# Sum of reciprocals: one row's reciprocal as a power on GpSimd

## The chip, the cores and the metric

The kernel runs on one core of one Trainium2 chip (the other seven are not used). The metric is the device time of one execution in microseconds (us), smaller is better; the input of 67.1 MB is read from HBM once, and the result of 64 KB is written back. The engines are named as in the profile: PE (TensorE), DVE (VectorE), ACT (ScalarE), POOL (GpSimd), and SP, which only issues DMAs here.

## The reference

```python
def setup_inputs():
    batch, seq, dim = 32, 512, 1024
    return {"x": np.abs(np.random.randn(batch, seq, dim)).astype(np.float32) + 1e-6}

def reference(x):
    return np.sum(1.0 / x, axis=-1).astype(np.float32)
```

For each of the 16,384 rows of 1,024 positive fp32 numbers the sum of the reciprocals is wanted.

## The kernel before

The 16,384 rows lie on 128 partitions, 128 rows to a partition (F = 128), numbered 0 to 127 in the order of the work. "Row 1" is thus one tile of 128 x 1024, row 1 of each partition. The rows go through a ring of R = 46 slots in SBUF (`ring`, 4 KB of each partition for a slot); row r takes slot r % 46, so rows 46 and up have to wait until the row 46 earlier has been finished. Row 127 is cut in two halves, handled as pieces 127 and 128. The sums go into `sums`, 128 x 128, and to HBM in seven stores at the end.

The reciprocal is made in two steps: ScalarE's `Abs_reciprocal_sqrt` gives 1/sqrt(x), with the scale FIT, in place, and then some engine squares it and sums it over the row. There are several ways for the second step, and the kernel spreads the rows over them:

- Z: ScalarE squares the row and sums it by itself.
- G, then T: GpSimd multiplies the row by itself in place (L280), and VectorE sums it (`tensor_reduce`, L283).
- Q: VectorE multiplies and sums in one instruction (L240).
- B, later K and M: VectorE takes batch-norm statistics (L255), from which the sum of squares is worked out later.
- C: ScalarE squares the row without summing, and T sums it.
- U, P, L, E, R: the two halves of a row are added by PE into PSUM (U, L201) and multiplied by GpSimd (P, L194); ScalarE takes the inverse root of the product (L) and squares it (E, both L211); VectorE multiplies product and sum and adds up (R, L220). This uses 1/a + 1/b = (a + b) / (a b), and saves ScalarE half of the elements.

The order of all of this is written out by hand in the string PLAN. A token is a letter, a row, and `+n` for n rows at once: A0+2 is the inverse root of rows 0 and 1 on ScalarE, G1+3 the square of rows 1 to 3 on GpSimd, T2+2 the sums of rows 2 and 3. Dn loads the next n rows; all loads are issued from SP. Each engine handles its own tokens strictly in the order of PLAN. Waits between engines follow from `note`, which keeps a history of who read and wrote which part of which slot, and leaves out the waits that others imply. Before the plan, GpSimd gets EARLY = 13 idle instructions (`nop`).

At the front the first loads are D2, D12, D12, D9 and D11, which fill the 46 slots: rows 0 and 1, then 2 to 13, and so on. They are issued one right after the other. The next load, D10, stands in PLAN behind T6+4 and needs slots 0 to 9, so it waits until rows 0 to 9 are finished. ScalarE's queue begins A0+2, Z0, A2, A3, A4+3, A7, A8, A9; GpSimd's G1+3, G6+3, G9, G11; VectorE's T1, T2+2, T6+4. The identity matrix for PE is made on GpSimd by `make_identity` (masks.py) ahead of the plan; PE uses it first for U53.

Of the kernel before, what the change touches and what calls it, by code (L numbers as in the profile page):

```python
# [11 lines left out]
def kernel(  # L12
# [5 lines left out]
    nc = tc.nc  # L18
    f32 = mybir.dt.float32
    P = 128  # L20
    EARLY = 13
    D = 1024
    H = D // 2
    F = 128
# [14 lines left out]


    PLAN = """
        D2 D12 D12 D9 D11 A0+2 Z0 A2 A3 A4+3 G1+3 A7 A8 A9 G6+3 A10 T1 A11+3 T2+2 Z4 Z5 G9 Z10
        Z12 G11 T6+4 D10 A14 A15+2 G13 A17+3 G16 T11 T13 A20+4 G17 Q15 G19 T16+2 A24+2 G20 A26
        A27 G21 A28+2 G23+3 A30+2 T19+3 A32+3 Z14 D8 G26 C33 Z18 G27 Z22 Z29 G28 A35+2 G30+3
        T23+6 D8 A37+3 A40+4 G34+2 T30+2 A44+2 Z36 T32 G40 Z37 T33+3 D8 Z38 G44+2 U53@0 A46+2
# [33 lines left out]
    pool = ctx.enter_context(tc.tile_pool(name="pool", bufs=1))  # L79
# [6 lines left out]
    stat_rows = [i for lo, step, n in STATS for i in range(lo, lo + step * n, step)]  # L86
    stats = pool.tile([P, len(stat_rows), 2, 2, 3], f32)
    ident = pool.tile([P, P], f32)
    ps = pspool.tile([P, 8, H], f32)
    make_identity(nc, ident)  # L90

    def parse(tok):
        body, _, b = tok[1:].partition("@")
        r, _, n = body.partition("+")
        return tok[0], int(r), int(n or 1), int(b or 0)

    def place(u):
        return (u, 0, D) if u < NR else PIECES[u - NR]

    def area(u, n=1):  # L100
        r, at, w = place(u)
        if u >= NR:
            w, n = sum(place(i)[2] for i in range(u, u + n)), 1
        return ring[:, r % R : r % R + n, at : at + w]
# [36 lines left out]
    def rows(u, n=1):  # L141
        spaces = []
        for r, at, w in (place(i) for i in range(u, u + n)):
            spaces += [("row", r % R, i) for i in range(at, at + w, 128)]
        return spaces
# [12 lines left out]
    with tc.manual_schedule():  # L158
        for _ in range(EARLY):
            nc.gpsimd.nop(hint="idle", nofuse=True)  # L160
        for op, u, n, b in (parse(tok) for tok in PLAN):
            if op == "D":
                n, u = u, loaded
                while n:
                    r, at, w = place(u)
                    m = min(n, R - r % R, NR - u, HALF - r % HALF) if u < NR else n
                    k = m
                    if u >= NR:
                        w, k = sum(place(i)[2] for i in range(u, u + m)), 1
                    inst = nc.sync.dma_start(  # L170
                        out=area(u, m),
                        in_=x_v[r // HALF, :, r % HALF : r % HALF + k, at : at + w],
                    )
                    note("SP", inst, writes=rows(u, m))
                    u, n = u + m, n - m
                loaded = u
            elif op in "AC":
                inst = nc.scalar.activation(  # L178
                    out=area(u, n),
                    in_=area(u, n),  # L180
                    func=Arsqrt if op == "A" else Square,
                    scale=FIT if op == "A" else 1.0,
                )
                note("ACT", inst, writes=rows(u, n))
            elif op == "Z":
                r = place(u)[0]
                inst = nc.scalar.activation(  # L187
                    out=area(u), in_=area(u), func=Square, accum_out=sums[:, r : r + 1]
                )
                summed.add(r)  # L190
                note("ACT", inst, writes=rows(u))
            elif op == "P":
                slot[u], r = b, u % R
                inst = nc.gpsimd.tensor_tensor(  # L194
                    out=prod[:, b], in0=ring[:, r, :H], in1=ring[:, r, H:], op=mult
                )
                note("POOL", inst, rows(u), [("slot", b)])
            elif op == "U":
                bank[u], r = b, u % R
                for h in range(2):  # L200
                    inst = nc.tensor.matmul(  # L201
                        ps[:, b],
                        lhsT=ident,
                        rhs=ring[:, r, h * H : (h + 1) * H],
                        start=h == 0,
                        stop=h == 1,
                    )
                    note("PE", inst, half(u, h * H), [("bank", b)])
            elif op in "LE":
                pair = prod[:, slot[u]]  # L210
                inst = nc.scalar.activation(  # L211
                    out=pair,
                    in_=pair,
                    func=Arsqrt if op == "L" else Square,
                    scale=S * FIT if op == "L" else 1.0,
                )
                note("ACT", inst, writes=[("slot", slot[u])])
            elif op == "R":
                pair = prod[:, slot[u]]
                inst = nc.vector.tensor_tensor_reduce(  # L220
                    out=pair,
                    in0=pair,
                    in1=ps[:, bank[u]],
                    scale=S,
                    scalar=0.0,
                    op0=mult,
                    op1=add,
                    accum_out=sums[:, u : u + 1],
                )
                note("DVE", inst, [("bank", bank[u])], [("slot", slot[u])])  # L230
            elif op == "Q":
                r, at, w = place(u)
                joined = [u]
                while len(joined) < n:
                    joined += [i for i in range(NR, u) if place(i)[0] == r][-len(joined) :][:1]
                at -= sum(place(i)[2] for i in joined[1:])
                w += sum(place(i)[2] for i in joined[1:])
                row = ring[:, r % R, at : at + w]
                total = sums[:, r : r + 1]
                inst = nc.vector.tensor_tensor_reduce(  # L240
                    out=row,
                    in0=row,
                    in1=row,
                    scale=1.0,
                    scalar=total if r in summed else 0.0,
                    op0=mult,
                    op1=add,
                    accum_out=total,
                )
                summed.add(r)  # L250
                note("DVE", inst, writes=[s for i in joined for s in rows(i)])
            elif op == "B":
                i = stat_rows.index(u)
                for h in range(2):
                    inst = nc.vector.bn_stats(  # L255
                        out=stats[:, i, h], in_=ring[:, u % R, h * H : (h + 1) * H]
                    )
                    note("DVE", inst, reads=half(u, h * H), writes=[("stat", i)])
            elif op in "KM":
                lo, step, n = STATS[u]  # L260
                i = stat_rows.index(lo)
                part = stats[:, i : i + n]
                if op == "K":
                    mean = part[:, :, :, :, 1].rearrange("p f h e -> p (f h e)")
                    inst = nc.scalar.activation(  # L265
                        out=mean, in_=mean, func=Square, scale=float(H // 2) ** 0.5
                    )
                    engine = "ACT"
                else:
                    inst = nc.vector.tensor_reduce(  # L270
                        out=sums[:, lo : lo + step * (n - 1) + 1 : step],
                        in_=part[:, :, :, :, 1:].rearrange("p f h e k -> p f (h e) k"),
                        axis=mybir.AxisListType.XY,
                        op=add,
                    )
                    engine = "DVE"
                note(engine, inst, writes=[("stat", j) for j in range(i, i + n)])
            elif op == "G":
                row = area(u, n)
                inst = nc.gpsimd.tensor_tensor(out=row, in0=row, in1=row, op=mult)  # L280
                note("POOL", inst, writes=rows(u, n))
            elif op == "T":
                inst = nc.vector.tensor_reduce(  # L283
                    out=sums[:, u : u + n],
                    in_=area(u, n),
                    axis=mybir.AxisListType.X,
                    op=add,
                )
                note("DVE", inst, reads=rows(u, n))
            elif op == "O":  # L290
                for lo, hi in zip(STORES, STORES[1:]):
                    store(lo, hi)
        store(STORES[-1], F)
# [30 lines left out]
```

## Time and profile before

| what | value |
|---|---|
| median of 2 runs | 166.24 us (166.18 to 166.3) |
| span of the profiled execution, first to last instruction | 164.2 us |
| ACT busy | 145.7 us (89%) in 148 instructions |
| DVE busy | 115.9 us (71%) in 147 instructions |
| POOL busy | 108.8 us (66%) in 56 instructions |
| PE busy | 38.2 us (23%) in 68 matmuls |
| input queue | 67.18 MB, 96.3% of the span of 16 DMA engines |
| mean granted TensorE clock | 0.952 |

The span is what the profile can explain; the time of a run is some 2 us longer, since it also holds what lies before the first and after the last instruction. The busy time of an engine is summed over its instructions; the idle instructions (`nop`), semaphore waits and the issuing of DMAs are not counted as busy. A row of the timeline gives the start, the duration, the engine, the line of the code, the operation, output and input tile with their shapes, the number of instructions merged in it, and in brackets how long the engine idled before it and which engine's work ended that.

### The profile page before, as it was taken

What the parts mean: (1) busy time and instruction counts of PE and PEld (TensorE: products, weight loads), DVE (VectorE), ACT (ScalarE), POOL (GpSimd) and SP (SyncE); (2) the same over time, 40 slices, a digit from 0 to 9 for tenths busy, and PEclk for the clock granted to TensorE, in tenths of its full rate; (3) what the DMA queues carried; (4) which work ended last, traced back from release to release, by engine and by line L of the source; (5) the groups of instructions that cost most, each with busy time, mean ns of one, the idle gap of its engine ahead of it and who ended that gap; (6) DMA issues with size and microseconds to landing.
All of it is one profiled execution on the core that took longest, in us unless ns stands there. A gap on an engine that the chain in (4) does not pass through costs nothing.

```text
span 164.2 us, 640 instructions
## 1 busy us (share of the span) xinstructions
PE 38.2 (23%) x68; PEld 14.4 (9%) x68; DVE 115.9 (71%) x147; ACT 145.7 (89%) x148; POOL 108.8 (66%) x56
## 2 busy tenths in 40 slices
PE   0000000000000000053000000065908198699700
PEld 0000000000000000020000000032302033234200
DVE  0000003559927039999999999999698969999894
ACT  3600199999999999999999999999999999999994
POOL 1000069998999999999507979999926195477300
PEclk9999999999999999999999999999975859999985
DMA  5999899899989899999998998999999999999970
GB/s 188 463 539 407 383 395 563 383 431 431 463 351 527 351 479 409 391 455 431 391 503 383 431 463 381 455 407 441 419 425 467 414 419 422 421 411 417 408 249 2
DMA packets 4611, 67.20 MB, mean 409 GB/s; under 512 B 1408, under 2 KB 1408, under 8 KB 2176
## 3 DMA queue, kind: packets, MB, share of 16 engines
q1 hardware_dynamic: 4608, 67.18, 96.3%
q14 instruction: 3, 0.02, 0.0%
HBM read 67.11 MB, written 0.07 MB: 409 GB/s over the span
## 4 chain that ended last, share of the span: by engine, by line
ACT 63%; DMA 26%; DVE 6%; issue 2%; POOL 2%; SPq 0%; DVEq 0%; POOLq 0%
ACT ring L178 47%; DMA ring<-in_x_dram 26%; ACT ring L187 10%; ACT prod L211 6%; DVE ring L240 2%; DVE stats L255 2%; POOL prod L194 2%; DVE prod L220 1%; DVE sums L283 0%; SPq L170 0%; ACT stats L265 0%; DVE sums L240 0%; DVE sums L220 0%; DVEq L240 0%; POOLq L194 0%
## 5 line engine op out<-in xcount | busy, mean ns | idle before, releaser
L178 ACT ACTIVATE ring<-ring 128x1024 f32<-128x1024 f32 (+4 forms) x65 | 104.1, 1658 | 15.2 <-DMA ring<-in_x_dram 15.1
L280 POOL TENSOR_TENSOR ring<-ring 128x1024 f32<-128x1024 f32 (+2 forms) x33 | 85.9, 2634 | 29.9 <-ACT ring L178 29.9
L283 DVE TENSOR_REDUCE sums<-ring 128x1 f32<-128x1024 f32 (+4 forms) x27 | 53.3, 1999 | 42.2 <-POOL ring L280 42.1
L201 PE MATMUL ps<-ring,ident 128*128 128x512 f32 x68 | 38.2, 712 | 117.2 <-DMA ring<-in_x_dram 115.9
L255 DVE BATCH_NORM_STATS2 stats<-ring 128x6 f32<-128x512 f32 x58 | 36.5, 679 | 3.1 <-ACT ring L178 3.1
L194 POOL TENSOR_TENSOR prod<-ring 128x512 f32<-128x512 f32 x17 | 22.5, 1339 | 15.0 <-DMA ring<-in_x_dram 10.8
L201 PEld LDWEIGHTS ps<-ring,ident 128*128 128x128 f32 x68 | 14.4, 224 | 140.2 <-POOL ring L280 71.6
L187 ACT ACTIVATE ring<-ring 128x1024 f32<-128x1024 f32 x23 | 23.9, 1041 | 0.0
L211 ACT ACTIVATE prod<-prod 128x512 f32<-128x512 f32 x34 | 19.8, 615 | 0.2
L240 DVE CUSTOM_DVE_ANT_0 ring<-ring 128x1024 f32<-128x1024 f32 (+1 forms) x12 | 17.6, 1480 | 0.5 <-ACT ring L178 0.4
L220 DVE CUSTOM_DVE_ANT_0 prod<-prod,ps 128x512 f32<-128x512 f32 x17 | 11.1, 676 | 0.1
L187 ACT ACTIVATION_READ_ACCUMULATOR ring<-ring 128x1 f32 x23 | 4.3, 187 | 0.0
L70 ACT ACT_TABLE_LOAD x1 | 1.3, 1283 | 0.7 <-PEq L308 0.7
L220 DVE DVE_READ_ACCUMULATOR2_ANT sums<- 128x1 f32 x17 | 1.4, 81 | 0.0
L240 DVE DVE_READ_ACCUMULATOR2_ANT sums<- 128x1 f32 x13 | 1.0, 81 | 0.0
L240 DVE CUSTOM_DVE_ANT_0 ring<-ring,sums 128x512 f32<-128x512 f32 x1 | 0.8, 752 | 0.1
masks.py:199 POOL TENSOR_SCALAR_AFFINE_SELECT ident<-ident 128x128 f32<-128x128 f32 x1 | 0.3, 293 | 0.5 <-POOL ident masks.py:197 0.5
L265 ACT ACTIVATE stats<-stats 128x44 f32<-128x44 f32 (+1 forms) x2 | 0.5, 272 | 0.0
L270 DVE TENSOR_REDUCE sums<-stats 128x11 f32<-128x88 f32 (+1 forms) x2 | 0.5, 264 | 0.0
masks.py:197 POOL MEMSET ident<- 128x128 f32 x1 | 0.2, 205 | 0.3 <-POOLq L308 0.3
L308 POOL MEMSET const-float32-0.0<- 128x1 f32 x1 | 0.1, 99 | 0.2 <-issue 0.2
L308 POOL MEMSET const-bfloat16-1.0<- 128x1 bf16 x1 | 0.1, 102 | 0.0
(2 smaller groups left out, 0.2 us busy)
## 6 DMA issues: line engine op xcount, KB each, us to landing
ring<-in_x_dram SPq DMA_DIRECT2D x2, 6144.0 KB, 25.8
ring<-in_x_dram SPq DMA_DIRECT2D x3, 4096.0 KB, 26.0
ring<-in_x_dram SPq DMA_DIRECT2D x3, 3072.0 KB, 26.3
ring<-in_x_dram SPq DMA_DIRECT2D x1, 5632.0 KB, 55.9
ring<-in_x_dram SPq DMA_DIRECT2D x1, 5120.0 KB, 32.4
ring<-in_x_dram SPq DMA_DIRECT2D x1, 4608.0 KB, 43.3
ring<-in_x_dram SPq DMA_DIRECT2D x4, 1024.0 KB, 37.8
ring<-in_x_dram SPq DMA_DIRECT2D x1, 3584.0 KB, 24.4
```

Source lines behind the costliest of these rows:

```text
L70: nc.scalar.add_instruction(mybir.InstLoadActFuncSet(name=nc.get_next_instruction_name(), act_func_set_id=act_sets.index("abs_reciprocal_s ...
L178: inst = nc.scalar.activation(out=area(u, n), in_=area(u, n), func=Arsqrt if op == "A" else Square, scale=FIT if op == "A" else 1.0,)
L187: inst = nc.scalar.activation(out=area(u), in_=area(u), func=Square, accum_out=sums[:, r : r + 1])
L194: inst = nc.gpsimd.tensor_tensor(out=prod[:, b], in0=ring[:, r, :H], in1=ring[:, r, H:], op=mult)
L201: inst = nc.tensor.matmul(ps[:, b], lhsT=ident, rhs=ring[:, r, h * H : (h + 1) * H], start=h == 0, stop=h == 1,)
L211: inst = nc.scalar.activation(out=pair, in_=pair, func=Arsqrt if op == "L" else Square, scale=S * FIT if op == "L" else 1.0,)
L220: inst = nc.vector.tensor_tensor_reduce(out=pair, in0=pair, in1=ps[:, bank[u]], scale=S, scalar=0.0, op0=mult, op1=add, accum_out=sums[:, ...
L240: inst = nc.vector.tensor_tensor_reduce(out=row, in0=row, in1=row, scale=1.0, scalar=total if r in summed else 0.0, op0=mult, op1=add, acc ...
L255: inst = nc.vector.bn_stats(out=stats[:, i, h], in_=ring[:, u % R, h * H : (h + 1) * H])
L265: inst = nc.scalar.activation(out=mean, in_=mean, func=Square, scale=float(H // 2) ** 0.5)
L280: inst = nc.gpsimd.tensor_tensor(out=row, in0=row, in1=row, op=mult)
L283: inst = nc.vector.tensor_reduce(out=sums[:, u : u + n], in_=area(u, n), axis=mybir.AxisListType.X, op=add,)
```

## The change

Row 1 leaves ScalarE and the square on GpSimd. A new token W raises it, in place, to the power -1 on GpSimd: a `tensor_tensor` with the ALU operation `pow`, whose second operand is a new tile `minus`, 128 x 1024, filled with -1.0 by a memset on GpSimd ahead of the identity matrix. A0+2 becomes A0, and G1+3 becomes G2+2; T1, which sums row 1, is as before and now reads what W1 wrote. W1 stands in PLAN behind Z0, and it is GpSimd's first token. EARLY is 11 in place of 13.

```diff
-    EARLY = 13
+    EARLY = 11
...
     PLAN = """
-        D2 D12 D12 D9 D11 A0+2 Z0 A2 A3 A4+3 G1+3 A7 A8 A9 G6+3 A10 T1 A11+3 T2+2 Z4 Z5 G9 Z10
+        D2 D12 D12 D9 D11 A0 Z0 W1 A2 A3 A4+3 G2+2 A7 A8 A9 G6+3 A10 T1 A11+3 T2+2 Z4 Z5 G9 Z10
...
     ident = pool.tile([P, P], f32)
+    minus = pool.tile([P, D], f32)
+    nc.gpsimd.memset(minus, -1.0)
     ps = pspool.tile([P, 8, H], f32)
     make_identity(nc, ident)
...
+            elif op == "W":
+                row = area(u)
+                inst = nc.gpsimd.tensor_tensor(
+                    out=row, in0=row, in1=minus, op=mybir.AluOpType.pow
+                )
+                note("POOL", inst, writes=rows(u))
             elif op == "G":
```

## The prediction

> **What bounds the kernel now.** I read the page first: the span and the busy slices.
>
> ```profile
> span 164.2 us, 640 instructions
> ...
> ACT  3600199999999999999999999999999999999994
> POOL 1000069998999999999507979999926195477300
> ...
> DMA  5999899899989899999998998999999999999970
> ```
>
> Each digit is the busy share of one fortieth of the span, 4.1 us. The DMA row is full from the second slice to the last but two: the input streams without a hole. ACT is full from the sixth slice on. POOL has a hole of almost five slices at the front, one near the middle, and a thin end. So two things set the time together, the input stream and ACT, and POOL sets it only if it falls so far behind that one of them waits. The chain of waits, followed back from the last instruction, says the same (start, duration, what):
>
> ```profile
> 1.17 18.77 DMA ring<-in_x_dram
> 19.94 0.02 issue
> 19.97 11.09 ACT ring L178 x8
> ...
> 99.43 24.43 DMA ring<-in_x_dram
> ```
>
> POOL's own steps come into it late only. Then the timeline of the front, where the change lies (start, duration, engine, work, in brackets the idle time before and who ended it):
>
> ```profile
> 5.48 1.91 ACT L178 ACTIVATE ring<-ring 128x2048 f32<-128x2048 f32 x1 [3.46 <-DMA ring<-in_x_dram]
> ...
> 19.97 11.09 ACT L178 ACTIVATE ring<-ring 128x1024 f32<-128x1024 f32 x8 [11.40 <-DMA ring<-in_x_dram]
> 22.05 10.57 POOL L280 TENSOR_TENSOR ring<-ring 128x3072 f32<-128x3072 f32 x2 [20.31 <-ACT ring L178]
> 27.39 3.41 DVE L283 TENSOR_REDUCE sums<-ring 128x1 f32<-128x1024 f32 x2 [27.39 <-POOL ring L280]
> ```
>
> Rows 0 and 1 are there at 5.48. ACT handles them (A0+2, then Z0) and then waits 11.40 us for rows 2 to 13. POOL's first piece, G1+3, waits for ACT's A3 and starts at 22.05. DVE's T1 and T2+2 follow G1+3 at 27.39. The prices of the shapes, by group (count | busy us, mean ns | idle):
>
> ```profile
> L280 POOL TENSOR_TENSOR ring<-ring 128x1024 f32<-128x1024 f32 x24 | 47.2, 1987 | 8.7 <-ACT ring L178 8.7
> ...
> L178 ACT ACTIVATE ring<-ring 128x1024 f32<-128x1024 f32 x36 | 36.4, 1041 | 11.6 <-DMA ring<-in_x_dram 11.6
> L178 ACT ACTIVATE ring<-ring 128x2048 f32<-128x2048 f32 x15 | 28.3, 1895 | 3.6 <-DMA ring<-in_x_dram 3.5
> ...
> L280 POOL TENSOR_TENSOR ring<-ring 128x3072 f32<-128x3072 f32 x4 | 21.2, 5306 | 20.3 <-ACT ring L178 20.3
> ...
> L280 POOL TENSOR_TENSOR ring<-ring 128x2048 f32<-128x2048 f32 x5 | 17.9, 3601 | 0.9 <-ACT ring L178 0.9
> ...
> masks.py:197 POOL MEMSET ident<- 128x128 f32 x1 | 0.2, 205 | 0.3 <-POOLq L308 0.3
> ...
> L308 POOL MEMSET const-float32-0.0<- 128x1 f32 x1 | 0.1, 99 | 0.2 <-issue 0.2
> ```
>
> Last, how far POOL may fall behind, from the timeline further on and from the list of waits:
>
> ```profile
> 39.02 98.58 SPq L170 DMA_DIRECT2D ring<-in_x_dram  x17
> 40.69 35.33 POOL L280 TENSOR_TENSOR ring<-ring 128x1024 f32<-128x1024 f32 x13 [0.66 <-ACT ring L178]
> ...
> 75.98 2.25 POOL L194 TENSOR_TENSOR prod<-ring 128x512 f32<-128x512 f32 x1
> ...
> 80.09 0.61 ACT L211 ACTIVATE prod<-prod 128x512 f32<-128x512 f32 x1
> ```
>
> ```profile
> PE ps L201 <- DMA ring<-in_x_dram: 115.9, 7, 71.6
> ...
> ACT ring L178 <- DMA ring<-in_x_dram: 15.1, 3, 11.4
> ```
>
> From 22.05 on, POOL idles 0.66 us ahead of 40.69 and then runs without a gap to the end of P53 at 75.98 + 2.25 = 78.23. ACT takes P53's result (L53) at 80.09, so that POOL has 1.86 us to spare there. ACT's three waits for data are 3.46, 11.40 and 0.23 us: 15.1 in all, nearly all of it ahead of 19.97.
>
> **The change, part by part.**
>
> *ACT.* A0+2 over two rows (1.90 us by its group) becomes A0 over one (1.04). The 0.86 us saved lie ahead of ACT's wait of 11.40 us, which the arrival of rows 2 to 13 ends: Z0 ends earlier, the wait is 12.26 us, A2 still starts at 19.97. Gain on the path: 0. Were that wait gone, it would be 0.86.
>
> *The constant.* One memset of 1,024 elements on POOL. From 128 elements in 205 ns and one element in 99 ns, an element costs (205 - 99) / 127 = 0.83 ns, so I estimate 99 + 1,023 x 0.83 = 0.95 us. It stands ahead of the identity matrix, whose first reader is PE after a wait of 71.6 us, and ahead of W1, which can't start before 5.48. Hidden; without that cover 0.95.
>
> *The two idle instructions fewer.* They lie in POOL's hole of 20.31 us, ahead of the wait that ends it. Cost 0 either way.
>
> *POOL's square.* G1+3 (5.31 us) becomes G2+2 (3.60): 1.71 us less of POOL work. G2+2 still waits for A3, so it starts at 22.05, if POOL is free by then. POOL would be 1.71 us ahead, T2+2 and T6+4 on DVE up to as much earlier, and so would the load D10, which SP issues at 39.02 when T6+4 has freed its slots. But at 40.69 POOL waits for ACT already, so its lead ends there at the latest; and the loads queue behind a stream that is full, so an earlier issue moves no byte forward. Gain: 0.
>
> *T1.* It waits for W1 in place of G1+3 and comes earlier as long as W1 ends before 27.36.
>
> *W1 itself, the unknown.* It needs the load of rows 0 and 1, so it starts at about 5.48. Behind it in POOL's queue stands G2+2, and behind that all of POOL's work; T1 on DVE waits for it too, with T2+2 behind. The room: POOL is free at 22.05 if W1 lasts up to 16.57 us. Up to 16.57 + 1.71 = 18.28 us POOL is no later than before. Up to 18.28 + 0.66 + 1.86 = 20.80 us L53 on ACT still finds P53 done. Above that ACT stops at L53 and has no idle time left to win it back: one for one. A loss of 2%, 3.3 us, needs W1 at 24.1 us.
>
> The trace has no power on any engine. The nearest row is the multiply of the same engine and shape, 1.99 us: the lower end, as the power reads two operands and writes one just as the multiply does. For the upper end I count arithmetic: x to the power y as a logarithm, a product and an exponential, each by a short series, is some 20 steps. If each of them cost a whole multiply pass over a further row, (5306 - 1987) / 2 = 1,660 ns, that makes 20 x 1.66 = 33.2 us. [...] I take a third of a pass for a step and one pass for the traffic: 20 x 0.55 + 1.66 = 12.7 us. That is an estimate with a weak base; it is nearer to the multiply's row than to the upper end, and both ends stay for the range. At 12.7 us W1 runs from 5.5 to 18.2, ends 3.9 us before POOL is needed, and the sum of the change is 0.
>
> First calls are a further question. POOL's first tensor_tensor, at 22.05, belongs to a group of four whose mean is 5.31 us, and two in a row from 22.05 took 10.57: the first one paid nothing extra. [...]
>
> **The sum.** The span stays at 164.2 us. The median of two runs is 166.24 us, 2.0 above the span of the profiled execution, for what lies around it. So 166.2.
>
> **The rivals.**
>
> *The power is too long for the hole (slower).* Its place is POOL's queue between 5.5 and 22; its price is W1 less 20.8 us; it decides from 24.1 us on. At the upper end, 20 steps of a whole pass each because a step waits for the one before, W1 takes 33 us: 166.2 + 33.2 - 20.8 = 178.6. For it: nothing in the trace bounds the power at 12 multiplies, 24.1 / 1.99. [...] Would the input stream run dry first? Two loads tell:
>
> ```profile
> ring<-in_x_dram SPq DMA_DIRECT2D x1, 5632.0 KB, 55.9
> ring<-in_x_dram SPq DMA_DIRECT2D x1, 5120.0 KB, 32.4
> ```
>
> The first is the last load of the front, which lands 55.9 us after its issue at the kernel's start; the second is D10, issued at 39.02. D10 could go out at least 55.9 - 39.0 = 16.9 us later before the stream has a hole, and at W1 = 33.2 POOL is 33.2 - 18.3 = 14.9 late. So ACT's stop comes first. [...]
>
> *POOL's lead reaches the end (a little faster).* If the wait at 40.69 moved with the rest and every later step kept its lead, the most would be G1+3's 1.71 us: 164.5. Against it: that wait is for ACT, which hasn't moved, and the DMA row is full. It is within 2% in any case. Nothing that the change takes away adds up to 3.3 us: 0.86 + 1.71 = 2.57.
>
> *The power isn't run as one GpSimd instruction of this shape.* Then POOL's row count and the time of W1 would differ; with anything shorter than 20.8 us the result is again 166.2.
>
> **How the numbers follow.** W1 under 20.8 us and nothing moves: 0.52. The lead reaches the end: 0.03. W1 between 20.8 and 24.1: 0.03. W1 between 24.1 and 33: 0.20. W1 beyond 33: 0.19. Something that I don't see and that helps by over 2%: 0.03. Measured against 2%, about what a measurement of this kernel can tell from no change, this makes faster 0.03, same 0.58, slower 0.39. The forecast is that of the likeliest case, 166.2, whose own range is 165.2 to 167.2. The range for 8 in 10 leaves out W1 beyond 33 and reaches from 165.2 to 178.6.
>
> **What would show it.** In the profile after, one 128x1024 tensor_tensor of a new line on POOL at about 5.5 us carries the verdict. If it ends before 22, G2+2 (128x2048) must start at 22.05 on ACT's release, ACT's wait ahead of 19.97 must read about 12.3 us, POOL must wait for ACT again near 40.7, and the end must not move. If it is longer than 20.8 us, POOL's idle time ahead of G2+2 is gone, T1 and T2+2 are late, and ACT has a new wait for POOL at L211 near 80 us of the length W1 less 20.8. I am wrong if the end moves by over 1 us though W1 fits, or if W1 doesn't fit and ACT doesn't wait.

## The result, and the profile after

| kernel | median | span of the profiled execution |
|---|---|---|
| before | 166.24 us | 164.2 us |
| changed | 310.21 us (310.15 to 310.28, 2 runs) | 308.3 us |

The change makes the kernel 1.867 times as long (95% interval 1.861 to 1.872). The span and what lies around it (1.9 us, 2.0 before) say that the whole loss lies inside the span. The page of the changed kernel, busy tenths by fortieths of the span, now 7.7 us each:

```profile
span 308.3 us, 640 instructions
...
ACT  4049999993000000000000000180099979999996
POOL 4999999999999999999999999999939998459620
...
DMA  8999999400000000000000009995999999999800
```

The input stream, which had no hole before, stands still for 16 slices, and ACT for 15, a little later. POOL is full from the second slice to the 29th. The start of the chain of waits names what fills it (start, duration, what):

```profile
0.74 4.72 DMA ring<-in_x_dram
5.53 163.63 POOL ring L282
169.16 31.76 POOL ring L288 x13
200.92 1.79 issue
202.72 1.90 POOL ring L288
204.64 14.26 DVE sums L291 x5
```

L282 is W1, one single instruction. The front of the timeline, which answers to the one quoted from before:

```profile
0.73 0.95 POOL L90 MEMSET minus<- 128x1024 f32 x1 [0.29 <-POOLq L316]
...
5.48 1.06 ACT L180 ACTIVATE ring<-ring 128x1024 f32<-128x1024 f32 x1 [3.46 <-DMA ring<-in_x_dram]
5.53 163.63 POOL L282 TENSOR_TENSOR ring<-ring,minus 128x1024 f32<-128x1024 f32 x1 [3.34 <-DMA ring<-in_x_dram]
...
20.02 11.09 ACT L180 ACTIVATE ring<-ring 128x1024 f32<-128x1024 f32 x8 [12.30 <-DMA ring<-in_x_dram]
```

W1 starts where it should, at 5.53, and lasts 163.63 us, nearly as long as the whole span before, 164.2 us. Who waited for whom, in total, times, and longest:

```profile
DVE sums L291 <- POOL ring L282: 169.2, 1, 169.2
ACT ring L180 <- DMA ring<-in_x_dram: 142.6, 3, 126.9
...
ACT prod L213 <- POOL prod L196: 15.7, 1, 15.7
...
ACT stats L267 <- DVE stats L257: 1.9, 1, 1.9
```

T1 on VectorE waits for W1 to its end; behind it T2+2 and T6+4 are late, so D10 goes out at 184.40 in place of 39.02, the slots stay taken until then, and ScalarE runs out of rows: 126.9 us for data, then 15.7 us at L53 for P53, then 1.9 us at K0 (L267) for VectorE.

### The profile page after: what moved, and what is told of

It reads as the page before. It is cut to its first block, busy times and chain, and to the rows that moved or that the text cites. A ratio compares the mean times of both kernels' runs of the same rounds, so it can differ in the third digit from the quotient of the medians.

```text
span 308.3 us, 640 instructions
## 1 busy us (share of the span) xinstructions
PE 40.1 (13%) x68; PEld 15.3 (5%) x68; DVE 116.1 (38%) x147; ACT 144.9 (47%) x148; POOL 273.0 (89%) x58
## 4 chain that ended last, share of the span: by engine, by line
POOL 64%; DVE 16%; ACT 16%; DMA 2%; issue 1%; DVEq 0%
POOL ring L282 53%; POOL ring L288 11%; DVE sums L291 9%; ACT ring L180 9%; ACT prod L213 5%; DVE stats L257 4%; DVE ring L242 3%; ACT ring L189 2%; DMA ring<-in_x_dram 2%; DVE prod L222 0%; ACT stats L267 0%; DVE sums L242 0%; DVEq L242 0%; DVE sums L222 0%; DVEq L327 0%
## 5 line engine op out<-in xcount | busy, mean ns | idle before, releaser
L180 ACT ACTIVATE ring<-ring 128x1024 f32<-128x1024 f32 (+4 forms) x65 | 103.3, 1646 | 142.6 <-DMA ring<-in_x_dram 142.6
L282 POOL TENSOR_TENSOR ring<-ring,minus 128x1024 f32<-128x1024 f32 x1 | 163.6, 163634 | 3.3 <-DMA ring<-in_x_dram 3.3
L288 POOL TENSOR_TENSOR ring<-ring 128x1024 f32<-128x1024 f32 (+2 forms) x33 | 84.8, 2601 | 14.9 <-ACT ring L180 14.9
L203 PE MATMUL ps<-ring,ident 128*128 128x512 f32 x68 | 40.1, 745 | 249.4 <-POOL ring L288 199.1
L203 PEld LDWEIGHTS ps<-ring,ident 128*128 128x128 f32 x68 | 15.3, 238 | 273.4 <-POOL ring L288 199.0
L213 ACT ACTIVATE prod<-prod 128x512 f32<-128x512 f32 x34 | 19.7, 617 | 15.8 <-POOL prod L196 15.7
L196 POOL TENSOR_TENSOR prod<-ring 128x512 f32<-128x512 f32 x17 | 23.3, 1392 | 3.0 <-DMA out_dram<-sums 1.7
L189 ACT ACTIVATE ring<-ring 128x1024 f32<-128x1024 f32 x23 | 23.9, 1041 | 0.0
L242 DVE CUSTOM_DVE_ANT_0 ring<-ring 128x1024 f32<-128x1024 f32 (+1 forms) x12 | 18.3, 1534 | 0.0
L267 ACT ACTIVATE stats<-stats 128x44 f32<-128x44 f32 (+1 forms) x2 | 0.6, 282 | 1.9 <-DVE stats L257 1.9
L90 POOL MEMSET minus<- 128x1024 f32 x1 | 1.0, 951 | 0.3 <-POOLq L316 0.3
L242 DVE DVE_READ_ACCUMULATOR2_ANT sums<- 128x1 f32 x13 | 1.0, 80 | 0.0
L242 DVE CUSTOM_DVE_ANT_0 ring<-ring,sums 128x512 f32<-128x512 f32 x1 | 0.8, 751 | 0.1
## 6 DMA issues: line engine op xcount, KB each, us to landing
ring<-in_x_dram SPq DMA_DIRECT2D x1, 5120.0 KB, 14.5
```

The source lines that it names most:

```text
L180: inst = nc.scalar.activation(out=area(u, n), in_=area(u, n), func=Arsqrt if op == "A" else Square, scale=FIT if op == "A" else 1.0,)
L189: inst = nc.scalar.activation(out=area(u), in_=area(u), func=Square, accum_out=sums[:, r : r + 1])
L196: inst = nc.gpsimd.tensor_tensor(out=prod[:, b], in0=ring[:, r, :H], in1=ring[:, r, H:], op=mult)
L203: inst = nc.tensor.matmul(ps[:, b], lhsT=ident, rhs=ring[:, r, h * H : (h + 1) * H], start=h == 0, stop=h == 1,)
L213: inst = nc.scalar.activation(out=pair, in_=pair, func=Arsqrt if op == "L" else Square, scale=S * FIT if op == "L" else 1.0,)
L242: inst = nc.vector.tensor_tensor_reduce(out=row, in0=row, in1=row, scale=1.0, scalar=total if r in summed else 0.0, op0=mult, op1=add, acc ...
```

## The experiments

All runs below stand beside runs of the kernel before on the same chip, whose medians were 166.03 to 166.06 us.

### A multiply in the power's place

```diff
-                    out=row, in0=row, in1=minus, op=mybir.AluOpType.pow
+                    out=row, in0=row, in1=minus, op=mult
```

> W1 multiplies row 1 by the tile of -1.0 in place of raising it to that power; all else is as in the changed kernel (row 1's sum is then minus the sum of x). Theory 'the power's own duration is the whole loss': W1 takes about 1.9 us, starts at 5.5, G2+2 starts at 22.05 again, time 166.2 (within 0.5). Rival 'the second operand's tile, the wait of GpSimd for the first load, or the order at the front costs something by itself': the time stays well above 166, up to 310.

Measured: 166.0 us, ratio 0.9995 (0.9985 to 1.0004). POOL's timeline of this run:

```profile
5.50 2.35 POOL L282 TENSOR_TENSOR ring<-ring,minus 128x1024 f32<-128x1024 f32 x1 [3.31 <-DMA ring<-in_x_dram]
22.03 3.60 POOL L288 TENSOR_TENSOR ring<-ring 128x2048 f32<-128x2048 f32 x1 [14.18 <-ACT ring L180]
26.58 7.16 POOL L288 TENSOR_TENSOR ring<-ring 128x3072 f32<-128x3072 f32 x2 [0.95 <-ACT ring L180]
```

The tile of -1.0, the wait for the load, the two idle instructions and the new order cost nothing together. The operation alone is the loss. The multiply itself took 2.35 us, not the 1.9 expected. The 1.71 us that POOL is ahead begin to melt at 26.58 already, where it waits for ACT again.

### The power of 128, 256 and 112 columns

```diff
-                row = area(u)
+                row = ring[:, u % R, :128]
                 inst = nc.gpsimd.tensor_tensor(
-                    out=row, in0=row, in1=minus, op=mybir.AluOpType.pow
+                    out=row, in0=row, in1=minus[:, :128], op=mybir.AluOpType.pow
```

The other two runs have 256 and 112 in place of 128.

> The power is taken of the first 128 of row 1's 1,024 columns only; the other 896 stay x. Theory 'the power costs by the element, 163.6 us / 1,024 = 160 ns for each column': W1 takes 20.5 us, ends at 26.0, which is under the 20.8 us that the prediction's sum allows, so 166.2 (up to 166.6), although G2+2 starts 4 us late. Rival 'a cost of the first call, code loading for one, that doesn't grow with the row': W1 takes over 100 us and the time is near 300.

> The power is taken of 256 columns; the other 768 stay x. Theory 'by the element': W1 takes 40.9 us, and the kernel loses 40.9 - 20.8 = 20.1, one for one: 186.3. Rival 'first call': near 300. Rival 'the loss begins elsewhere than at 20.8 us, because the load D10 and not L53 is what POOL's delay stops first': a time that lies off 186.3 by more than 2 us.

The third was chosen after these two:

> The power is taken of 112 columns; the other 912 stay x. By the runs on 128, 256 and 1,024 columns (20.8, 41.2, 163.6 us) W1 takes 0.4 + 112 x 0.159 = 18.3 us and ends at 23.8, so that POOL is as late as before the change: 1.75 us past 22.05, against the 1.71 that G2+2 saves. Theory 'what fits ends at 18.3 + 0.66 = 18.9 us, since behind it VectorE's T23+6 starts late and VectorE has no idle time left': 166.1 (within 0.3), against 167.8 with 128 columns. Rival 'any time past 22.05 is lost': 166.1 + 1.75 = 167.8.

Measured: 167.79 us with 128 columns, ratio 1.0104 (1.0089 to 1.0119); 187.74 with 256, ratio 1.1305 (1.1286 to 1.1324); 166.07 with 112, ratio 1.0000 (0.9991 to 1.0010). First the timeline of the kernel before at two steps that the sum will need, VectorE's T23+6 and ScalarE's K0, and the busy time of its engines from 66 to 107 us (of 41.00 us, in the order PE, PEld, DVE, ACT, POOL, with the number of instructions; then the granted clock, the DMA share and GB/s):

```profile
59.97 6.55 DVE L283 TENSOR_REDUCE sums<-ring 128x6 f32<-128x6144 f32 x1 [7.47 <-POOL ring L280]
...
107.89 0.25 ACT L265 ACTIVATE stats<-stats 128x44 f32<-128x44 f32 x1
```

```profile
66.00:107.00 41.00, 3.75 (x4) 1.17 (x4) 40.73 (x44) 40.77 (x33) 33.10 (x13) 1.00 0.99 425
```

Then the timelines of the runs with 128, 256 and 112 columns, that with 256 followed by two of its waits:

```profile
5.56 20.79 POOL L282 TENSOR_TENSOR ring<-ring,minus 128x128 f32<-128x128 f32 x1 [3.37 <-DMA ring<-in_x_dram]
26.32 8.87 POOL L288 TENSOR_TENSOR ring<-ring 128x2048 f32<-128x2048 f32 x2
...
61.83 6.55 DVE L291 TENSOR_REDUCE sums<-ring 128x6 f32<-128x6144 f32 x1 [7.46 <-POOL ring L288]
...
80.17 0.61 ACT L213 ACTIVATE prod<-prod 128x512 f32<-128x512 f32 x1
...
109.60 0.27 ACT L267 ACTIVATE stats<-stats 128x44 f32<-128x44 f32 x1 [1.82 <-DVE stats L257]
```

```profile
5.50 41.25 POOL L282 TENSOR_TENSOR ring<-ring,minus 128x256 f32<-128x256 f32 x1 [3.31 <-DMA ring<-in_x_dram]
46.72 3.60 POOL L288 TENSOR_TENSOR ring<-ring 128x2048 f32<-128x2048 f32 x1
...
76.51 8.25 ACT L180 ACTIVATE ring<-ring 128x2048 f32<-128x2048 f32 x5 [4.47 <-DMA ring<-in_x_dram]
...
82.22 6.55 DVE L291 TENSOR_REDUCE sums<-ring 128x6 f32<-128x6144 f32 x1 [7.46 <-POOL ring L288]
```

```profile
ACT prod L213 <- POOL prod L196: 15.7, 1, 15.7
...
ACT stats L267 <- DVE stats L257: 1.9, 1, 1.9
```

```profile
5.43 18.26 POOL L282 TENSOR_TENSOR ring<-ring,minus 128x112 f32<-128x112 f32 x1 [3.24 <-DMA ring<-in_x_dram]
23.66 16.27 POOL L288 TENSOR_TENSOR ring<-ring 128x2048 f32<-128x2048 f32 x6
```

The cost is by the column: (163.63 - 41.25) / 768 = 159.4 ns, and (41.25 - 20.79) / 128 = 159.8 ns. What is left besides the columns is 20.79 - 128 x 0.1594 = 0.4 us, so a cost that doesn't grow with the row is at most that.

What fits is about 19 us, not 20.8. With 112 columns W1 takes 18.26 us, G2+2 starts 1.6 us late, and nothing is lost. With 128 columns W1 takes 20.79 us, just inside the prediction's 20.80, and 1.74 us are lost, which puts the limit at 19.05; the 18.9 in the expectation is a sum. The rows show the way: T23+6 on VectorE starts 61.83 - 59.97 = 1.86 us late, VectorE has next to no idle time behind it (40.73 of 41 us busy in the kernel before), and ScalarE, which took L53 at 80.17 without a wait, waits 1.82 us at K0 for VectorE.

With 256 columns T23+6 is 22.25 us late, and 187.74 - 166.05 = 21.7 us are lost, 1.4 more than expected. ScalarE's waits say where. It waits 4.47 us for data at 76.51 (its other waits for data are those of the front), 15.7 us for P53 at L53, and 1.9 us at K0. The first two make 20.2 us, and W1 less the prediction's 20.8 is 20.45; K0 adds its 1.9 us as with 128 columns. The changed kernel has the same split: 126.9 + 15.7 = 142.6 us up to L53, against 163.6 - 20.8 = 142.8, and 1.9 us at K0. There T23+6 is 204.64 - 59.97 = 144.7 us late, and 144.0 are lost. The delay of T23+6 gives the loss within 0.7 us in all three.

### ScalarE's K0 later

```diff
-         ... D2 K0 U81@1 A80 A82+2 G79 M0 B80 ... T78+2 Z75
-         G83 L81 Z76 D2 P85@2 B84 U89@3 ...
+         ... D2 U81@1 A80 A82+2 G79 B80 ... T78+2 Z75 K0
+         G83 L81 Z76 D2 P85@2 B84 M0 U89@3 ...
```

> The run with 128 columns (the other 896 stay x), with ScalarE's step K0 and VectorE's M0, which work out the first batch-norm sums, moved some 4 us later in the plan. In the run with 128 columns POOL is 1.9 us late, P53 is in time for ScalarE's L53 all the same, VectorE's T23+6 starts 1.86 us late, and ScalarE waits 1.8 us for VectorE at K0; the loss was 1.74 us. Theory 'the late work passes from POOL over VectorE to ScalarE at K0, and by nothing else': 166.1 to 166.5. Rival 'VectorE's lateness goes into the freeing of slots too, and the loads or the end are late anyway': 167.3 to 167.9.

Measured: 166.12 us, ratio 1.0005 (0.9996 to 1.0015). VectorE's row in this run:

```profile
61.87 6.55 DVE L291 TENSOR_REDUCE sums<-ring 128x6 f32<-128x6144 f32 x1 [7.46 <-POOL ring L288]
```

T23+6 is as late as with 128 columns before, 1.90 us. Of ScalarE's waits in this run none of over 0.2 us is at K0 (L267), where it was 1.82, and the loss is gone to within 0.1 us. So at this size the delay went into the time through K0 (moved together with M0). In a plan in which K0 stands later, a W1 of 20.79 us fits; how much longer it could be there wasn't tried.

### POOL's lead without the power

```diff
-        D2 D12 D12 D9 D11 A0+2 Z0 A2 A3 A4+3 G1+3 A7
+        D2 D12 D12 D9 D11 A0+2 Z0 G1 A2 A3 A4+3 G2+2 A7
```

> No power: the kernel before with G1+3 split, so that GpSimd squares row 1 by itself in its idle time (A0+2 Z0 G1 ... G2+2). It computes the full reference. This is the gain that the change was left with if W1 had cost nothing. Theory 'POOL's lead of 1.7 us ends at its wait for ACT near 40.7 and the input stream is full': 166.2 (within 0.3). Rival 'the lead reaches the end': 164.5.

Measured: 166.05 us, ratio 1.0001 (0.9992 to 1.0011). POOL's timeline:

```profile
7.39 1.89 POOL L280 TENSOR_TENSOR ring<-ring 128x1024 f32<-128x1024 f32 x1 [5.66 <-ACT ring L178]
21.97 3.60 POOL L280 TENSOR_TENSOR ring<-ring 128x2048 f32<-128x2048 f32 x1 [12.69 <-ACT ring L178]
26.51 7.16 POOL L280 TENSOR_TENSOR ring<-ring 128x3072 f32<-128x3072 f32 x2 [0.95 <-ACT ring L178]
```

GpSimd can square row 1 in its idle time, and that is worth nothing. Together with the run of the multiply, which also has ScalarE's shorter A0, it says that the most that the change could have given was zero.

### The reciprocal on VectorE

```diff
-                inst = nc.gpsimd.tensor_tensor(
-                    out=row, in0=row, in1=minus, op=mybir.AluOpType.pow
-                )
-                note("POOL", inst, writes=rows(u))
+                inst = nc.vector.reciprocal(out=row, in_=row)
+                note("DVE", inst, writes=rows(u))
```

> Row 1's reciprocal is made by VectorE's reciprocal in its idle time at the front in place of GpSimd's power (the full reference is computed; the tile of -1.0 stays, unused). VectorE is idle until 27.4. Theory 'the front's idle engines have nothing to give, since the kernel is held by the input stream and ScalarE from 20 us on': W1 takes under 22 us on VectorE and the time is 166.1 (within 0.3). Rival 'the idea was good and only the engine was wrong': below 165.5.

Measured: 166.12 us, ratio 1.0000 (0.9990 to 1.0010). VectorE's timeline:

```profile
5.46 6.55 DVE L282 RECIPROCAL ring<-ring 128x1024 f32<-128x1024 f32 x1 [5.46 <-DMA ring<-in_x_dram]
12.04 1.22 DVE L289 TENSOR_REDUCE sums<-ring 128x1 f32<-128x1024 f32 x1
```

The same result for row 1 takes 6.55 us on VectorE, a 25th of GpSimd's power, and fits its idle time with room to spare: from the end of T1 to 25.69 VectorE idles for another 12.42 us. The time stays where it was.

### What the power's price depends on: the exponent, the partitions

```diff
-    nc.gpsimd.memset(minus, -1.0)
+    nc.gpsimd.memset(minus, 1.0)
```

> The tile of exponents holds 1.0 in place of -1.0, so row 1 stays x. Theory 'the power goes one general way (logarithm, product, exponential) whatever the exponent': W1 takes 163.6 us within 2%, time 310. Rival 'exponents that are whole numbers, or negative ones, have a way of their own': W1 changes by over 10%.

```diff
-                row = area(u)
+                row = ring[:8, u % R, :]
                 inst = nc.gpsimd.tensor_tensor(
-                    out=row, in0=row, in1=minus, op=mybir.AluOpType.pow
+                    out=row, in0=row, in1=minus[:8], op=mybir.AluOpType.pow
```

The second run of this kind has 64 in place of 8.

> The power is taken of row 1 on partitions 0 to 7 only (1,024 columns); the other 120 partitions keep x in row 1. [...] Rival 'a column is one vector of long arithmetic': W1 takes 163.6 us as before. In both the time is 166.2 + W1 less what fits, 18.9 us: 229 or 311.

> The power is taken of row 1 on partitions 0 to 63 only; the other 64 keep x in row 1. Theory 'the partitions are shared out over cores that work side by side': W1 takes 163.6 us as for all 128, time 311. Rival 'one after the other over all 128 partitions': W1 takes 82 us, time 229.

Measured: 310.15 us with the exponent 1, 329.65 with 8 partitions, 334.12 with 64 (one run each). W1 with the exponent 1, then W1 and VectorE's Q15 (L242) with 8 partitions and with 64, then Q15 in the changed kernel, all from the timelines:

```profile
5.49 163.64 POOL L282 TENSOR_TENSOR ring<-ring,minus 128x1024 f32<-128x1024 f32 x1 [3.30 <-DMA ring<-in_x_dram]
```

```profile
5.47 163.63 POOL L282 TENSOR_TENSOR ring<-ring,minus 8x1024 f32<-8x1024 f32 x1 [3.27 <-DMA ring<-in_x_dram]
...
186.41 32.47 DVE L242 CUSTOM_DVE_ANT_0 ring<-ring 128x1024 f32<-128x1024 f32 x1
```

```profile
5.34 163.63 POOL L282 TENSOR_TENSOR ring<-ring,minus 64x1024 f32<-64x1024 f32 x1 [3.15 <-DMA ring<-in_x_dram]
...
186.28 37.38 DVE L242 CUSTOM_DVE_ANT_0 ring<-ring 128x1024 f32<-128x1024 f32 x1
```

```profile
186.47 1.86 DVE L242 CUSTOM_DVE_ANT_0 ring<-ring 128x1024 f32<-128x1024 f32 x1
```

W1 takes the same 163.6 us for x to the 1 and x to the -1, and on 8, 64 and 128 partitions. Of what was varied only the number of columns counts. In what order or by what units the partitions of a column are handled, on which the 82 and 229 us of the expectations rested, no run shows; W1 took 163.63 us with 8 partitions and with 64. The times of the two runs with fewer partitions were missed by 19 and 23 us, and Q15 explains it: it is 30.6 and 35.5 us longer than in the changed kernel. VectorE's next two waits for POOL there, 3.28 and 7.46 us, are gone in these runs, which leaves 19.9 and 24.8 us, against 19.4 and 23.9 us of longer time. The last section comes back to Q15.

## Why the prediction was wrong, point by point

*The step that failed* is the sentence "I take a third of a pass for a step and one pass for the traffic", and with it the upper end of 33.2 us. The mechanism of the slower rival was right in its place, POOL's queue between 5.5 and 22, and in its price, W1 less what fits. By its formula the measured W1 gives 166.2 + 163.6 - 20.8 = 309.0 us, against 310.21 measured; the wait at K0, 1.9 us, which it left out, covers what is missing. But W1 was put at 12.7 us, and it took 163.6, which is 99 multiply passes of 1.66 us. Twenty steps at a full pass each looked like a bound from above and weren't one: it counted the steps of a textbook, and nothing in the trace tied the instruction to that count. No run shows that the power has 20 steps, or that a step costs a third of a pass (0.55 us) and the traffic one: these were the author's estimates, and in their place the runs show 159.4 ns for each column. The chance of 0.19 for anything beyond 33 us was the honest part of it, and far too small for a term without a row.

*What fits: 18.28 us before POOL is later than before.* Shown, by 112 columns: 18.26 us, no loss.

*What fits: 20.80 us before the end moves.* Wrong by about 1.8 us. For what it looked at, POOL's own queue up to ScalarE's L53, the sum holds: with a W1 of 20.79 us L53 doesn't wait, and with longer ones ScalarE waits W1 less 20.8 up to there, within 0.3 us. It left out VectorE, which waits for POOL at T23+6 and, in the profile of before, is busy for 40.7 of the 41 us from 66 to 107. The step that it holds up is K0 on ScalarE. With K0 later, a W1 of 20.79 us costs nothing.

*"So ACT's stop comes first."* At the measured size it doesn't: the load D10 goes out 145.4 us late, the stream stands still, and ScalarE waits 126.9 us for data before its 15.7 us at L53. So the new wait at L53 isn't W1 less 20.8, as the prediction's sign has it; that is the sum of the two waits. The condition in the prediction (a hole in the stream once D10 is 16.9 us late) allows for that, and the run with 256 columns, where D10 goes out at 61.98 and so 23.0 us late, shows that wait begin, with 4.47 us; the size was off again.

*What was costed at zero.* ScalarE's wait became 12.30 us (predicted 12.26) and A2 started at 20.02 in place of 19.97; the memset took 951 ns (predicted 0.95 us) and lies in idle time; the multiply in the power's place shows all of this together at no cost. The two idle instructions weren't varied by themselves.

*POOL's lead is worth nothing.* Shown, by the run that squares row 1 early. The lead begins to go before 40.7 already: POOL waits 0.95 us for ACT ahead of 26.51, and by 40.62 it starts as late as it did before (40.69).

*The first call, and the steps of a power.* No cost of a first call shows in W1: 128 columns took 20.79 us, of which the columns explain all but 0.4, and in the changed kernel W1 starts 0.05 us after ScalarE's A0, which waits for the same load (5.53 and 5.48). No run shows what the steps of a power are.

## What to carry to other kernels

An operation that has no row in the trace is not bounded by the rows of cheaper ones (163.6 us here, against the multiply's 1.99): if the sign of the answer hangs on its price, run it once by itself on a narrow tile and read the slope from two widths, as 128 and 256 columns did here to 0.3%. Idle time at the front of an engine is worth filling only if that engine, or one that waits for it, sets the end later; here it was free and worth nothing (166.05 and 166.12 us, against 166.03 to 166.06). And to find how late an engine may be, follow each engine that waits for it to its next wait, not only the engine's own queue.

## What the runs showed of the hardware that was not expected

GpSimd's power costs 159.4 ns for each column, whatever the exponent (1 or -1) and however many partitions take part; the multiply in its place, with the same two operands, took 2.35 us where the power takes 163.6.

When W1 worked on 8 or 64 partitions only, Q15 on VectorE, which reads two operands from SBUF, took 32.47 and 37.38 us where it takes 1.86 us after a W1 on all 128. In all three runs GpSimd went through its squares without a gap for some 51 us from 169 on, so a busy GpSimd alone doesn't do it. The eleven Q rows of this shape sum up to 48.2 and 52.7 us, against 17.6, which is Q15's own difference within half a microsecond; with 8 partitions Q42 became shorter (1.21 us, against 2.96) and the other nine together longer (14.5 us, against 12.8). GpSimd falls idle at 222.58 in the run with 64 partitions and at 223.71 in the run with 8; Q15 ends 1.1 us behind the first and 4.8 us ahead of the second.

The cause wasn't tried, and no run here shows it.
